# Four direct feed-forward pairs, block sums on DVE, SSD state updates in the second feed-forward block

## The chip, the cores and the metric

The kernel runs on one core of a Trainium2 chip. The metric is the device time of one execution in microseconds (us), as the median of several runs of the same program. Six engines with queues of their own matter: PE (matrix products, with PEld for its weight loads), DVE, ACT and POOL (elementwise work), and SP, which issues nearly all DMAs here. Each engine takes its instructions strictly in order and stands still at a wait.

## The reference

One step of a hybrid decoder layer on 512 prompt tokens and 8 sequences of 4 new tokens (544 columns in all), width 1024:

```python
x = x + 0.5 * swiglu(rmsnorm(x, n_f1), w_f1u, w_f1d)        # swiglu: (silu(g) * u) @ w_down, D_FF = 2816
m, new_conv, new_ssm, new_hg = mixer(rmsnorm(x, n_mix), ...)  # SSD heads and HGRN2 heads, then @ w_out
x = x + m
x = x + 0.5 * swiglu(rmsnorm(x, n_f2), w_f2u, w_f2d)
x = x + sigmoid(rmsnorm(x, n_ple) @ w_gate) * rmsnorm(p @ w_proj, ple_post)
y = rmsnorm(x, norm_final)
```

Beside `y` the new states come out. For the 8 sequences the new SSD state is h = h0 * decay + (sum of outer products of B and x), 2 groups x 8 sequences, each a tile of 128x512; the HGRN2 state is updated in the same way.

## The kernel before

Everything is kept transposed: 128 features on the partitions, 544 tokens in the free dimension, as two halves of 272. Every fp32 product is made of three matmuls (hi x hi, hi x lo, lo x hi). So an operand is first **cut**: ACT copies it to a rounded `hi` (line 245) and DVE subtracts to get `lo` (line 246). `body` runs `ffn` for the first block, the mixer, the W_o stage (lines 1169 to 1187), `ffn` for the second block, and a last gate.

**The feed-forward block (`ffn`, line 235)** has 22 gate/up pairs of 256 output features. A **direct pair** (`plain_mm`, line 330) takes 96 matmuls of 128x272, in four steps `kp` over K. All other pairs are made in a **period** (line 503) by seven products of sums of blocks, 84 matmuls (72 in the first period), at the price of sums and cuts of the weights (`w_s1` to `w_c4`) and of eight sums `t` of the input blocks. Before the change pairs 0 to 2 are direct and periods 3 to 21 follow. The input blocks `b` are x times the norm weight (`block`, line 314: a DVE `tensor_scalar` of 128x272 for each row block and half), cut into `bh`/`bl` (`put`; later ones are named `bx`). The eight sums `t` are made on POOL (lines 396 to 400), written behind pair 0. The tail of a direct pair (`plain_h`, line 365: scale, SiLU, two products, cut to `hh`/`hl`) is cut into steps that a table (`steps`, line 485) places in later work. The down products (`dn_run`, 24 matmuls) read `hh`/`hl` of four pairs at a time. In `ffn` the order on each engine is the order of the code (`pin`, line 62).

**In the W_o stage** 16 half slabs of 48 matmuls run. In the code, from the fourth half slab on, two or three state updates (lists `ups` and `begun`) are put between half slabs: 16 `ssm_update` (line 630: load `h0`, scale on POOL, mask `Bm` on DVE, one matmul of 128x512, add on DVE, store) and 16 `hg_update` (line 661, with `vb` on DVE ahead of its matmul). Here Tile's scheduler sets the order, and the first instructions of the second `ffn` can be mixed in.

## Time and profile before

| | us |
|---|---|
| median of 3 runs (1440.3 to 1443.42) | 1441.34 |
| the profiled execution | 1442.06 |
| its span (clock 0.983 of full speed on average) | 1440.2 |
| PE busy | 1386.6 (96%) |
| DVE busy | 1007.8 (70%) |
| ACT busy | 680.7 (47%) |
| POOL busy | 324.3 (23%) |

PE is busy nearly all the time, so the profile is read by its gaps: where PE stands still, what released it, and where its matmuls run at a lower granted clock. A timeline row is: start, duration, engine, line, operation, out<-in, count, and in brackets the idle time ahead and the releaser. On PE the first `ffn` runs from the start to about 399 us, the mixer to 835, the W_o stage to 951, the second `ffn` to about 1351.

### The profile page before, as it was taken

What the parts mean: (1) busy time and instruction counts of PE and PEld (TensorE: products, weight loads), DVE (VectorE), ACT (ScalarE), POOL (GpSimd) and SP (SyncE); (2) the same over time, 40 slices, a digit from 0 to 9 for tenths busy, and PEclk for the clock granted to TensorE, in tenths of its full rate; (3) what the DMA queues carried; (4) which work ended last, traced back from release to release, by engine and by line L of the source; (5) the groups of instructions that cost most, each with busy time, mean ns of one, the idle gap of its engine ahead of it and who ended that gap; (6) DMA issues with size and microseconds to landing.
All of it is one profiled execution on the core that took longest, in us unless ns stands there. A gap on an engine that the chain in (4) does not pass through costs nothing. (4 is left out here: it accounts for less than half of the span.)

```text
span 1440.2 us, 27177 instructions
## 1 busy us (share of the span) xinstructions
PE 1386.6 (96%) x11045; PEld 1340.8 (93%) x11045; DVE 1007.8 (70%) x1595; ACT 680.7 (47%) x1220; POOL 324.3 (23%) x285
## 2 busy tenths in 40 slices
PE   6989999999999999999999999979899999999997
PEld 6979999999999999999999799979799999999896
DVE  7687666666568887777775587785966666665465
ACT  5544444443443465555553373445444444343655
POOL 3243233232111100000001121233423223231100
PEclk9999999999999999999999999999999999999998
DMA  5223332332432422222222546762233233322311
GB/s 189 74 81 96 105 95 88 94 98 69 154 110 77 135 91 92 91 92 91 91 99 73 164 153 219 254 199 84 81 103 89 88 103 93 100 84 78 118 45 63
DMA packets 68191, 155.00 MB, mean 108 GB/s; under 512 B 8609, under 2 KB 15905, under 8 KB 68065
## 3 DMA queue, kind: packets, MB, share of 16 engines
q1 hardware_dynamic: 66480, 150.65, 33.1%
q10 hardware_dynamic: 1584, 2.61, 0.5%
q8 instruction: 87, 1.43, 0.4%
q14 instruction: 40, 0.32, 0.1%
HBM read 138.70 MB, written 14.52 MB: 106 GB/s over the span
## 5 line engine op out<-in xcount | busy, mean ns | idle before, releaser
L81 ACT CAST whi<-wraw 128x1024 fp32r<-128x1024 f32 (+2 forms) x140 | 132.5, 951 | 213.7 <-issue 85.7
L69 DVE TENSOR_TENSOR wlo<-wraw,whi 128x1024 fp32r<-128x1024 f32 (+2 forms) x140 | 161.5, 1157 | 92.0 <-ACT whi L81 87.8
L84 PE MATMUL ps_in<-xwh,whi 128*128 128x272 f32 x832 | 183.6, 297 | 0.0
L84 PE MATMUL ps_in<-xwh,wlo 128*128 128x272 f32 x832 | 175.5, 291 | 0.0
L84 PE MATMUL ps_in<-xwl,whi 128*128 128x272 f32 x832 | 173.5, 289 | 0.0
L84 PEld LDWEIGHTS ps_in<-xwh,whi 128*128 128x128 f32 x832 | 132.4, 188 | 8.5 <-issue 8.2
L81 ACT COPY s<-ps_s 128x272 f32<-128x272 f32 x114 | 43.7, 383 | 204.0 <-PE ps_s L84 204.0
L84 PEld LDWEIGHTS ps_in<-xwh,wlo 128*128 128x128 f32 x832 | 130.7, 189 | 2.9 <-issue 2.9
L84 PEld LDWEIGHTS ps_in<-xwl,whi 128*128 128x128 f32 x832 | 131.1, 189 | 1.5 <-issue 1.5
L69 POOL TENSOR_TENSOR wraw<-r,r 128x512 f32<-128x512 f32 x38 | 54.0, 1421 | 257.4 <-DVE r L69 257.4
L84 PE MATMUL ps_dn<-hl,dh 128*128 128x272 f32 x512 | 106.6, 290 | 3.8 <-DVE hl L69 3.8
L84 PE MATMUL ps_dn<-hh,dl 128*128 128x272 f32 x512 | 106.3, 289 | 0.1
L84 PE MATMUL ps_dn<-hh,dh 128*128 128x272 f32 x512 | 106.0, 288 | 0.0
L84 PE MATMUL ps_s<-bx,w3h 128*128 128x272 f32 x608 | 89.1, 289 | 7.2 <-ACT s L81 7.2
L84 PEld LDWEIGHTS ps_s<-bx,w3h 128*128 128x128 f32 x608 | 80.9, 188 | 8.2 <-ACT s L81 8.1
L84 PEld LDWEIGHTS ps_dn<-hl,dh 128*128 128x128 f32 x512 | 80.5, 189 | 4.3 <-DVE hl L69 4.3
L69 POOL TENSOR_TENSOR g<-g,r 128x544 f32<-128x544 f32 x38 | 67.3, 1772 | 63.7 <-ACT g L89 63.7
L84 PEld LDWEIGHTS ps_dn<-hh,dl 128*128 128x128 f32 x512 | 80.9, 189 | 0.5 <-DVE dl L69 0.5
L69 DVE TENSOR_TENSOR w3l<-r,w3h 128x1024 fp32r<-128x1024 f32 x40 | 51.3, 1282 | 42.1 <-ACT w3h L81 41.8
L84 PEld LDWEIGHTS ps_dn<-hh,dh 128*128 128x128 f32 x512 | 80.3, 189 | 0.0
L89 ACT ACT_TABLE_LOAD x55 | 70.6, 1283 | 3.3 <-DVE g L69 2.0
L69 POOL TENSOR_TENSOR s<-s 128x272 f32<-128x272 f32 x38 | 35.8, 943 | 117.7 <-ACT s L81 117.7
(381 smaller groups left out, 3605.1 us busy)
## 6 DMA issues: line engine op xcount, KB each, us to landing
wraw<-in_w_in SPq DMA_DIRECT2D x52, 512.0 KB, 3.3
r<-in_w1u SPq DMA_DIRECT2D x23, 512.0 KB, 4.3
r<-in_w2u SPq DMA_DIRECT2D x23, 512.0 KB, 4.4
dr<-in_w1d SPq DMA_DIRECT2D x32, 256.0 KB, 3.3
h<-in_hssm SPq DMA_DIRECT2D x32, 256.0 KB, 3.8
wraw<-in_w_o SPq DMA_DIRECT2D x16, 512.0 KB, 4.7
dr<-in_w2d SPq DMA_DIRECT2D x32, 256.0 KB, 3.3
wraw<-in_w1u SPq DMA_DIRECT2D x19, 256.0 KB, 3.3
```

The costliest lines, as they stand in the source:

```text
L69: pin((eng or V).tensor_tensor(out=out, in0=a, in1=b, op=op))
L81: pin(A.copy(out, a))
L84: pin(PE.matmul(out, w, x, **kw))
L89: ins = pin(A.activation(out=out, in_=in_, func=f, scale=scale, bias=bias, **kw))
```

## The change

Five edits, the first three in both feed-forward blocks:

1. Pair 3 is direct too: four direct pairs, then periods 4 to 21. Its weights are loaded ahead (`w3r`), and the tails of pairs 0 and 1 are finished within the direct part; those of pairs 2 and 3 lie in periods 4 and 5 (`steps`).
2. The eight sums `t` are made on DVE (`combo`), spread over pairs 1 and 2.
3. The second half of each block scaling is an ACT copy with a scale, the first stays on DVE.
4. `ssm_update` leaves the W_o stage, where one `hg_update` (once two) follows each half slab from the second on.
5. The SSD updates become a generator (`ssm_updates`) that the second `ffn` advances at four places of each period from 5 on (`aside`): load `h0`; scale by the decay (now on DVE) and `Bm`; the matmul; the add and the store.

```diff
@@ -234,3 +234,3 @@
 
-    def ffn(xs, nname, wu, wd, fp, ht, acc=None, load=None):
+    def ffn(xs, nname, wu, wd, fp, ht, acc=None, load=None, side=iter(())):
         pinned[0] = True
@@ -316,3 +316,7 @@
             for q in range(2):
-                ts(t[:, q], xs[2 * kp + q][:, half * HN:(half + 1) * HN], vc(nname, 2 * kp + q), ALU.mult)
+                src, n = xs[2 * kp + q][:, half * HN:(half + 1) * HN], vc(nname, 2 * kp + q)
+                if half:
+                    act(t[:, q], src, AF.Copy, scale=n)
+                else:
+                    ts(t[:, q], src, n, ALU.mult)
             blocks[kp, half] = t
@@ -383,3 +387,3 @@
             ks = slice(2 * kp, 2 * kp + 2)
-            b0, b1 = block(kp, 0), block(kp, 1)
+            b1, b0 = block(kp, 1), block(kp, 0)
             put(1 if kp < 2 else 2, kp % 2, b0)
@@ -395,7 +399,10 @@
             plain_mm(ps0, kp, w0h, w0l)
-        t = {(n, i): slot("t") for n, i in ((3, 1), (1, 0), (1, 1), (2, 0), (2, 1), (3, 0), (4, 0), (4, 1))}
-        for n, i in t:
-            x, y = {1: (blocks[i, 1], blocks[i, 0]), 2: (blocks[2 + i, 1], t[1, i]), 3: (blocks[i, 1], blocks[2 + i, 1]),
-                    4: (blocks[2 + i, 0], t[2, i])}[n]
-            tt(t[n, i], x, y, ALU.subtract, eng=G)
+        t = {}
+
+        def combo(n, i):
+            t[n, i] = slot("t")
+            x, y = {1: (blocks[i, 1], blocks[i, 0]), 2: (blocks[2 + i, 1], t.get((1, i))),
+                    3: (blocks[i, 1], blocks[2 + i, 1]), 4: (blocks[2 + i, 0], t.get((2, i)))}[n]
+            tt(t[n, i], x, y, ALU.subtract)
+
         w1h = [wtile(wp, "whi"), wtile(fp, "w3h", bufs=1)]
@@ -405,4 +412,6 @@
         w2r = [raw("r1", 8, 1), raw("r2", 8, 1)]
-        for q in range(2):
-            nc.sync.dma_start(w2r[q], wu[2][:, 8 * q:8 * q + 8])
+        w3r = [wp.tile([P, 8, P], F32, name="wraw", tag="wraw", bufs=2) for _ in range(2)]
+        for j, rw in ((2, w2r), (3, w3r)):
+            for q in range(2):
+                nc.sync.dma_start(rw[q], wu[j][:, 8 * q:8 * q + 8])
         done = [take(ps0, "g", None)]
@@ -410,2 +419,4 @@
         plain_mm(ps1, 0, w1h, w1l)
+        combo(1, 0)
+        combo(1, 1)
         if acc is None:
@@ -416,13 +427,14 @@
         plain_mm(ps1, 1, w1h, w1l)
-        put(5, 0, t[1, 0])
-        put(5, 1, t[1, 1])
         w2h = [wtile(wp, "whi") for _ in range(2)]
         w2l = [wtile(wp, "wlo") for _ in range(2)]
-        for q in range(2):
-            cut(w2r[q], w2h[q], w2l[q])
-        w_load(3)
+        cut(w2r[0], w2h[0], w2l[0])
+        combo(3, 0)
+        combo(3, 1)
+        cut(w2r[1], w2h[1], w2l[1])
         plain_mm(ps1, 2, w1h, w1l)
+        combo(2, 0)
+        combo(2, 1)
+        put(5, 0, t[1, 0])
+        put(5, 1, t[1, 1])
         plain_mm(ps1, 3, w1h, w1l)
-        put(6, 0, t[2, 0])
-        put(6, 1, t[2, 1])
         ps2 = two("ps_up")
@@ -433,8 +445,6 @@
         done.append(take(ps1, "g", None))
-        w_s1(3)
-        w_c2(3)
-        w_s3(3)
-        w_s4(3)
-        put(7, 0, t[3, 0])
-        put(7, 1, t[3, 1])
+        combo(4, 0)
+        combo(4, 1)
+        put(6, 0, t[2, 0])
+        put(6, 1, t[2, 1])
         pq = small()
@@ -444,8 +454,14 @@
         plain_mm(ps2, 1, w2h, w2l)
-        w_c1(3)
+        w3h = [wtile(wp, "whi"), wtile(fp, "w3h", bufs=1)]
+        w3l = [wtile(wp, "wlo"), wtile(fp, "w3l", bufs=1)]
+        cut(w3r[0], w3h[0], w3l[0])
+        put(7, 0, t[3, 0])
+        put(7, 1, t[3, 1])
         next(rg, None)
+        plain_mm(ps2, 2, w2h, w2l)
+        cut(w3r[1], w3h[1], w3l[1])
         put(4, 0, t[4, 0])
         put(4, 1, t[4, 1])
-        plain_mm(ps2, 2, w2h, w2l)
-        w_c3(3)
+        w_load(4)
+        plain_mm(ps2, 3, w2h, w2l)
         early = [plain_h(i, *done[i]) for i in range(2)]
@@ -453,5 +469,22 @@
             next(early[i % 2])
-        plain_mm(ps2, 3, w2h, w2l)
+        ps3 = [[small()[:, :HN] for _ in range(2)] for _ in range(2)]
+        plain_mm(ps3, 0, w3h, w3l)
         done.append(take(ps2, None, None))
         early.append(plain_h(2, *done[2]))
+        w_s1(4)
+        w_c2(4)
+        next(early[0])
+        next(early[1])
+        plain_mm(ps3, 1, w3h, w3l)
+        w_s3(4)
+        w_s4(4)
+        next(early[0])
+        next(early[1])
+        w_c1(4)
+        plain_mm(ps3, 2, w3h, w3l)
+        for i in (0, 1, 2, 2):
+            next(early[i])
+        plain_mm(ps3, 3, w3h, w3l)
+        done.append(take(ps3, None, None))
+        early.append(plain_h(3, *done[3]))
 
@@ -484,4 +517,4 @@
 
-        steps = {(3, 1): (0,), (3, 5): (0,), (3, 6): (0,), (4, 1): (1,), (4, 5): (1,), (4, 6): (1,), (4, 4): (2,),
-                 (4, 7): (2,), (5, 1): (2,), (5, 5): (2,), (5, 6): (2,)}
+        steps = {(4, 1): (2,), (4, 5): (2,), (4, 6): (2,), (4, 4): (3,), (4, 7): (3,), (5, 1): (3,), (5, 4): (3,),
+                 (5, 5): (3,)}
 
@@ -498,2 +531,6 @@
 
+        def aside(j):
+            if j > 4:
+                next(side, None)
+
         def gate(o):
@@ -517,2 +554,3 @@
                 gate(o)
+            aside(j)
             dn_out()
@@ -532,2 +570,3 @@
             dn_prep()
+            aside(j)
             product(a[:, :HN], w[6], X[6], False)
@@ -538,2 +577,3 @@
             dn_run()
+            aside(j)
             if j - 2 in GROUPS:
@@ -553,2 +593,3 @@
                 tail.append(last_slab(0))
+            aside(j)
             step(j, 5)
@@ -573,3 +614,3 @@
 
-        for j in range(3, NFF):
+        for j in range(4, NFF):
             period(j)
@@ -584,2 +625,3 @@
         ts_ = tail
+        aside(NFF)
         part(ts_[0], range(n - 1))
@@ -591,3 +633,7 @@
         h_parts(NFF - 1)
+        aside(NFF)
         part(ts_[1], range(n - 1))
+        aside(NFF)
+        for _ in side:
+            pass
         pinned[0] = False
@@ -629,6 +675,7 @@
 
-    def ssm_update(xp, g, b, st):
-        if b == 0:
-            xde = hs2(xp, "xde")
-            bkf = xp.tile([P, P], F32, name="bkf", tag="Bm", bufs=4)
+    def ssm_updates(fp, ht, tmp):
+        for g in range(2):
+            xde = ht("xde", F32)[:, :512]
+            bk = ht("bk", F32R)
+            bkf, Bh = f32(bk[:, :P]), bk[:, P:2 * P]
             for i in range(4):
@@ -636,25 +683,30 @@
                 nc.sync.dma_start(bkf[32 * i:32 * i + 32], bk_d[g])
-            xst = xp.tile([P, 512], F32R, name="xst", tag="xst", bufs=2)
-            Bk = xp.tile([P, P], F32, name="Bks", tag="Bks", bufs=2)
-            Bh = xp.tile([P, P], F32R, name="Bkh", tag="Bm", bufs=4)
-            A.copy(Bh, bkf)
-            A.copy(Bk, f32(Bh))
+            yield
+            yield
+            yield
+            xst = tmp()
+            Bk = fp.tile([P, P], F32, name="Bks", tag="Bks", bufs=1)
+            cp(Bh, bkf)
+            cp(xst, xde)
+            cp(Bk, f32(Bh))
+            tt(xst[64:], xde[64:], f32(xst[64:]), ALU.subtract)
             for i in (32, 96):
                 tt(Bk[i:i + 32], bkf[i:i + 32], f32(Bh[i:i + 32]), ALU.subtract)
-            A.copy(xst, xde)
-            tt(xst[64:], xde[64:], f32(xst[64:]), ALU.subtract)
-            st[g] = (xst, Bk)
-        xst, Bk = st[g]
-        h0 = hs2(xp, "h0")
-        nc.sync.dma_start(h0, hssm[g, b])
-        h3 = h0.rearrange("p (h q) -> p h q", q=64)
-        o = 64 + 16 * b + 8 * g
-        tt(h3, h3, cdk[:, o:o + 8].unsqueeze(2).to_broadcast([P, 8, 64]), ALU.mult, eng=G)
-        Bm = xp.tile([P, P], F32R, name="Bm", tag="Bm", bufs=4)
-        ts(Bm, Bk, cs("bmask")[:, b:b + 1], ALU.mult)
-        yield
-        pu = small()
-        PE.matmul(pu, Bm, xst, start=True, stop=True)
-        tt(h0, h0, pu, ALU.add)
-        nc.sync.dma_start(ssms_o[g, b], h0)
+            yield
+            for b in range(NB):
+                h0 = ht("h0", F32)[:, :512]
+                nc.sync.dma_start(h0, hssm[g, b])
+                yield
+                h3 = h0.rearrange("p (h q) -> p h q", q=64)
+                o = 64 + 16 * b + 8 * g
+                tt(h3, h3, cdk[:, o:o + 8].unsqueeze(2).to_broadcast([P, 8, 64]), ALU.mult)
+                Bm = fp.tile([P, P], F32R, name="Bm", tag="Bm", bufs=1)
+                ts(Bm, Bk, cs("bmask")[:, b:b + 1], ALU.mult)
+                yield
+                pu = small()
+                mm(pu, Bm, xst, start=True, stop=True)
+                yield
+                tt(h0, h0, pu, ALU.add)
+                nc.sync.dma_start(ssms_o[g, b], h0)
+                yield
 
@@ -1164,3 +1216,2 @@
                 for g in range(2):
-                    ups.append(lambda g=g, b=b: ssm_update(xp, g, b, st))
                     ups.append(lambda h=b, hf=g: hg_update(xp, h, hf, st))
@@ -1177,3 +1228,3 @@
                     next(g, None)
-                n = 0 if i < 3 else 3 - i % 2
+                n = 0 if i < 1 else 1 + (i == 8)
                 begun = [x() for x in ups[:n]]
@@ -1190,3 +1241,4 @@
         with tc.tile_pool(name="f2", bufs=1, reuse_waits="tile") as fp:
-            ffn(xs, "n_f2", w2u, w2d, fp, ring, acc2)
+            ffn(xs, "n_f2", w2u, w2d, fp, ring, acc2, side=ssm_updates(
+                fp, ring, lambda: xp2.tile([P, 512], F32R, name="xst", tag="sqa", bufs=1)))
 
```

DVE in the first `ffn`, from the last block of pair 0 to the cuts of pair 2's weights (`wlo<-r` and `w3l` are pair 1's and 2's weights, `sq` the squares for the norm), before:

```order
L69 TENSOR_TENSOR bl<-b,bh 128x544
L69 TENSOR_TENSOR wlo<-r_135,whi 128x1024
L69 TENSOR_TENSOR w3l<-r_139,w3h 128x1024
L69 TENSOR_TENSOR sq<-sq 128x544 x6
L69 TENSOR_TENSOR bl<-t,bh 128x544 x2
L69 TENSOR_TENSOR wlo<-r_319,whi 128x1024
L69 TENSOR_TENSOR wlo<-r_320,whi 128x1024
L69 TENSOR_TENSOR bx<-t,bx 128x544 x2
L69 TENSOR_TENSOR w5l<-r_420,w5h 128x512
```

and after the change:

```order
L69 TENSOR_TENSOR bl<-b,bh 128x544
L69 TENSOR_TENSOR wlo<-r_135,whi 128x1024
L69 TENSOR_TENSOR w3l<-r_139,w3h 128x1024
L69 TENSOR_TENSOR t<-b 128x544 x2
L69 TENSOR_TENSOR sq<-sq 128x544 x6
L69 TENSOR_TENSOR wlo<-r_303,whi 128x1024
L69 TENSOR_TENSOR t<-b 128x544 x2
L69 TENSOR_TENSOR wlo<-r_304,whi 128x1024
L69 TENSOR_TENSOR t<-b,t 128x544 x2
L69 TENSOR_TENSOR bl<-t,bh 128x544 x2
L69 TENSOR_TENSOR t<-b,t 128x544 x2
L69 TENSOR_TENSOR bx<-t,bx 128x544 x2
```

The sums `t`, which are POOL's before, stand between pair 1's squares and pair 2's weights, and the block scaling `b` is shorter.

DVE at the seam from the W_o stage to the second `ffn` (`xb<-ps_wo` are the last sums of the W_o stage, `s` and `h` the state updates, `vst`/`vb` the preparation of an `hg_update`; the rest is pair 0 of the second `ffn`), before:

```order
L69 TENSOR_TENSOR xb<-ps_wo,xb 128x544
L69 TENSOR_TENSOR s_11053<-s_11053,ps_s 128x512
L69 TENSOR_TENSOR h_11061<-h_11061,ps_s 128x512
L69 TENSOR_TENSOR sq<-sq 128x544
L69 TENSOR_TENSOR bl<-b,bh 128x544
L69 TENSOR_TENSOR vst<-vsf,vst 32x128 x2
L69 TENSOR_TENSOR vst<-vsf,vst 64x128
L69 TENSOR_TENSOR vb<-vst,cst 128x512
L69 TENSOR_TENSOR wlo<-wraw,whi 128x256
L69 TENSOR_TENSOR vb<-vst,cst 128x512
L69 TENSOR_TENSOR s_11076<-s_11076,ps_s 128x512
L69 TENSOR_TENSOR wlo<-wraw,whi 128x256
```

and after the change:

```order
L69 TENSOR_TENSOR xb<-ps_wo,xb 128x544
L69 TENSOR_TENSOR s_10907<-s_10907,ps_s 128x512
L69 TENSOR_TENSOR s_10974<-s_10974,ps_s 128x512
L69 TENSOR_TENSOR sq<-sq 128x544
L76 TENSOR_SCALAR b<-xb,vec 128x272
L69 TENSOR_TENSOR bl<-b,bh 128x544
L69 TENSOR_TENSOR wlo<-wraw,whi 128x256 x2
L69 TENSOR_TENSOR bl<-b,bh 128x544
L76 TENSOR_SCALAR b<-xb,vec 128x272 x2
L69 TENSOR_TENSOR bl<-b,bh 128x544
L69 TENSOR_TENSOR wlo<-wraw,whi 128x256 x2
L69 TENSOR_TENSOR bl<-b,bh 128x544
```

No update is prepared behind the last `xb` any more; two adds `s` are left, and what follows is all pair 0's.

DVE in the second `ffn`, one later period (`wlo<-wraw` is its c4 weights, `dl` a down slab), before:

```order
L69 TENSOR_TENSOR wlo<-wraw,whi 128x1024
L69 TENSOR_TENSOR dl<-dr,dh 128x512
L69 TENSOR_TENSOR g<-g,s_12026 128x272
L69 TENSOR_TENSOR g<-g,ps_s 128x272
L69 TENSOR_TENSOR hl<-g,hh 128x544
L69 TENSOR_TENSOR w5l<-r_12174,w5h 128x512
L69 TENSOR_TENSOR r_12260<-r_12174,r_12173 128x1024
L72 SCALAR_TENSOR_TENSOR xb<-ps_dn,xb 128x544
L69 TENSOR_TENSOR dl<-dr,dh 128x512
```

and after the change:

```order
L69 TENSOR_TENSOR wlo<-wraw,whi 128x1024
L69 TENSOR_TENSOR dl<-dr,dh 128x512
L69 TENSOR_TENSOR h_12184<-h_12184,cdk 128x512
L76 TENSOR_SCALAR Bm<-Bks,cst 128x128
L69 TENSOR_TENSOR g<-g,s_12022 128x272
L69 TENSOR_TENSOR g<-g,ps_s 128x272
L69 TENSOR_TENSOR hl<-g,hh 128x544
L69 TENSOR_TENSOR w5l<-r_12207,w5h 128x512
L69 TENSOR_TENSOR r_12298<-r_12207,r_12206 128x1024
L72 SCALAR_TENSOR_TENSOR xb<-ps_dn,xb 128x544
L69 TENSOR_TENSOR dl<-dr,dh 128x512
L69 TENSOR_TENSOR wlo<-r_12206,whi 128x1024
L69 TENSOR_TENSOR h_12184<-h_12184,ps_s 128x512
```

The scale and mask of an SSD update stand ahead of the products `g` of the pair before, and its add behind the cut of the next weights.

## Rows read from the trace of the kernel before

**Rows 1.** Waits of PE, whole span: line, waited for, us, times, longest.
```profile
PE ps_up L84 <- DVE bl L69: 9.8, 3, 4.3
...
PE ps_s L683 <- DVE vb L69: 6.2, 6, 1.7
```

**Rows 2.** Timeline of PE, first ffn, pair 0: start us, us, operation, [idle, releaser].
```profile
6.39 0.60 PE L84 MATMUL ps_up<-bh,whi 128*128 128x272 f32 x1 [6.39 <-ACT whi L81]
...
22.79 0.60 PE L84 MATMUL ps_up<-bl,whi 128*128 128x272 f32 x1 [4.08 <-DVE bl L69]
...
27.71 0.55 PE L84 MATMUL ps_s<-bh,whi 128*128 128x272 f32 x2
```

**Rows 3.** Timeline of DVE, first ffn, end of pair 0.
```profile
14.17 0.72 DVE L69 TENSOR_TENSOR bl<-b,bh 128x544 fp32r<-128x544 f32 x1
...
16.15 1.86 DVE L69 TENSOR_TENSOR bl<-b,bh 128x544 fp32r<-128x544 f32 x1 [0.17 <-ACT bh L81]
...
20.89 1.85 DVE L69 TENSOR_TENSOR bl<-b,bh 128x544 fp32r<-128x544 f32 x1
```

**Rows 4.** Timeline of POOL, first ffn, at the same time.
```profile
16.06 4.63 POOL L69 TENSOR_TENSOR t<-b 128x544 f32<-128x544 f32 x3 [15.08 <-DVE b L76]
```

**Rows 5.** Timeline of ACT, first ffn, start of the last K step of pair 0.
```profile
15.47 0.65 ACT L81 CAST bh<-b 128x544 fp32r<-128x544 f32 x1 [1.48 <-DVE b L76]
```

**Rows 6.** The page, part 5: a costly group of ACT.
```profile
L81 ACT COPY s<-ps_s 128x272 f32<-128x272 f32 x114 | 43.7, 383 | 204.0 <-PE ps_s L84 204.0
```

**Rows 7.** Windows: stretch, its us, busy us of each engine, granted clock, DMA share.
```profile
20.00:25.00 5.00, 2.21 (x10) 2.21 (x11) 5.00 (x4) 0.00 (x0) 5.00 (x4) 0.62 0.49 161
950.00:960.00 10.00, 6.30 (x39) 5.04 (x38) 9.81 (x20) 5.35 (x15) 1.82 (x2) 0.99 0.59 196
1060.00:1160.00 100.00, 100.00 (x798) 100.00 (x798) 67.36 (x85) 43.02 (x72) 31.16 (x24) 1.00 0.32 97
```

**Rows 8.** Timeline of PE, first ffn, periods 4 and 5.
```profile
65.80 0.67 PE L84 MATMUL ps_s<-bh,whi 128*128 128x272 f32 x4
...
76.86 1.27 PE L84 MATMUL ps_s<-bx,w3h 128*128 128x272 f32 x8 [1.88 <-ACT s L81]
...
81.41 0.77 PE L84 MATMUL ps_s<-bh,wlo 128*128 128x272 f32 x4 [1.77 <-DVE wlo L69]
...
92.17 1.26 PE L84 MATMUL ps_s<-bx,w3h 128*128 128x272 f32 x8 [0.95 <-ACT s L81]
...
97.89 0.52 PE L84 MATMUL ps_dn<-hl,dh 128*128 128x272 f32 x2 [1.91 <-DVE hl L69]
...
99.26 0.67 PE L84 MATMUL ps_s<-bh,whi 128*128 128x272 f32 x4
```

**Rows 9.** Timeline of PE, W_o stage to second ffn, pair 0 and start of pair 1.
```profile
950.63 0.39 PE L657 MATMUL ps_s<-xst,Bm 128*128 128x512 f32 x1
950.86 0.41 PE L84 MATMUL ps_up<-bh,whi 128*128 128x272 f32 x2
...
976.64 0.53 PE L84 MATMUL ps_s<-bh,whi 128*128 128x272 f32 x2
```

**Rows 10.** Timeline of PE, second ffn: start of period 4, end of the first down product.
```profile
1012.44 0.66 PE L84 MATMUL ps_s<-bh,whi 128*128 128x272 f32 x4
...
1046.89 0.43 PE L84 MATMUL ps_s<-bh,whi 128*128 128x272 f32 x1
```

**Rows 11.** Groups by form, 855 to 960: xcount | busy us, mean ns | idle before.
```profile
L69 DVE TENSOR_TENSOR h<-h,ps_s 128x512 f32<-128x512 f32 x16 | 11.0, 686 | 15.4 <-POOL h L69 7.5 <-issue 5.2 <-PE ps_s L657 2.8
...
L76 DVE TENSOR_SCALAR Bm<-Bks,cst 128x128 fp32r<-128x128 f32 x15 | 6.1, 414 | 0.0
...
L69 DVE TENSOR_TENSOR xst<-xde,xst 64x512 fp32r<-64x512 f32 x1 | 0.7, 690 | 0.0
```

**Rows 12.** Groups by form, 1060 to 1260, POOL.
```profile
L69 POOL TENSOR_TENSOR g<-g,r 128x544 f32<-128x544 f32 x12 | 22.1, 1846 | 8.7 <-ACT g L89 8.7
```

**Rows 13.** Timeline of DVE, second ffn, one steady period.
```profile
1166.83 1.23 DVE L69 TENSOR_TENSOR wlo<-wraw,whi 128x1024 fp32r<-128x1024 f32 x1 [2.21 <-ACT whi L81]
```

More of the change, by code (lines that the diff above doesn't have):

```diff
@@ L416, in ffn @@
         plain_mm(ps1, 1, w1h, w1l)
+        w2h = [wtile(wp, "whi") for _ in range(2)]
+        w2l = [wtile(wp, "wlo") for _ in range(2)]
+        cut(w2r[0], w2h[0], w2l[0])
+        combo(3, 0)
+        combo(3, 1)
+        cut(w2r[1], w2h[1], w2l[1])
+        plain_mm(ps1, 2, w1h, w1l)
+        combo(2, 0)
+        combo(2, 1)
         put(5, 0, t[1, 0])
         put(5, 1, t[1, 1])
-        w2h = [wtile(wp, "whi") for _ in range(2)]
-        w2l = [wtile(wp, "wlo") for _ in range(2)]
-        for q in range(2):
-            cut(w2r[q], w2h[q], w2l[q])
-        w_load(3)
-        plain_mm(ps1, 2, w1h, w1l)
         plain_mm(ps1, 3, w1h, w1l)
-        put(6, 0, t[2, 0])
-        put(6, 1, t[2, 1])
         ps2 = two("ps_up")
```

## The prediction

> **What bounds the kernel now.** I read the list of what PE waits for first, then PE's timeline around the longest waits, then the other engines at those times. In the steady periods there is nothing to win: from 1060 to 1160 us PE is busy 100.00 of 100 us with 798 matmuls at full clock, 0.1253 us each [rows 7]. That is the price of a matmul below, so a direct pair (96) is 12.0 us, a period (84) 10.5 us, a down product (24) 3.0 us. The time that can go lies at three kinds of place: the first direct pair of each block, where PE waits for DVE's `bl` (9.8 us in 3 waits), the state updates, where it waits for `vb` (6.2 us in 6) [rows 1], and the first periods, where it waits for what ends the direct pairs.
>
> Each wait costs twice. After a long one the matmuls go at half rate for a while: the granted clock in 20 to 25 us is 0.62 of full speed [rows 7], a mix of the levels 1.2 and 2.4 GHz. From 22.79 to 27.71 us, the last 22 matmuls of pair 0 take 4.92 us instead of 2.76 [rows 2].
>
> **A, first block, pair 0.** It runs from 6.39 to 27.71, with 4.08 us of waiting for `bl` ahead of 22.79 [rows 2]. DVE is the late one: its cut of 128x544 takes 0.72 at 14.17, but 1.86 and 1.85 at 16.15 and 20.89 [rows 3], and from 16.06 on POOL makes the sums `t` [rows 4]. An instruction that takes 2.6 times as long while POOL works on SBUF is a shared resource. The Trainium skill (SBUF — State Buffer, Who interferes with whom) says that a DVE instruction with two SBUF inputs and a POOL instruction that reads SBUF use one port, and that the later one stands still until the other is done; 1.86 against 0.72 agrees. With the sums gone from POOL, the stretch from 16.15 to 22.74 (two `bl`, two weight cuts) shrinks to about 2.2 us (twice 0.72 and about 0.8), so the last `bl` is there near 18.4, just as PE gets to it (18.71). The wait of 4.08 goes, and with it the slow clock behind it, 4.92 - 2.76 = 2.16: **6.2 us**. Two of four block scalings move to ACT, a copy of 128x272 at 0.38 [rows 6], 0.77 for a K step; ACT stands 1.48 us per K step waiting for DVE's `b` [rows 5], so that is covered. If it isn't and half of the wait stays, the term is 3.1.
>
> The eight sums cost DVE 8 x about 0.65 = 5.2 us (an addition of 128x512 is 0.69 [rows 11], and back to back they overlap). They lie beside pairs 1 and 2, 24 us of matmuls, where DVE has two thirds of its time in use. I take them at nothing. Were they late, the cuts of pair 2 would be: up to 2 us.
>
> **B, the added matmuls.** A direct pair has 12 matmuls more than a period, twice: 24 x 0.1253 = **-3.0 us**, certain.
>
> **C, first block, first periods.** From the start of period 4 (65.80) to the end of the first down product (99.26) are 33.46 us [rows 8] for 84 + 84 + 24 = 192 matmuls, 24.06 us: 9.4 lost. Of these 1.88 + 1.77 + 0.95 + 1.91 = 6.5 are the waits [rows 8]; the other 2.9 are slow clock. The pattern: the tail of a direct pair stands on DVE and ACT ahead of what the period needs, so ACT's copy `s`, which frees PE for the period's last product, and the cut of the next weights come late. Two such periods are in this stretch. In the new code pairs 0 and 1 end inside the direct part, period 4 has no period before it (like period 3 now, which loses next to nothing), and only period 5 is like these two. It keeps a wait for `s` between 0.95 and 3.65 (1.88 + 1.77); I take the middle, 2.3. The wait for `hl` stays, but for pair 3 instead of 2, six matmuls (0.75) later in the down product: 1.2. Of the slow clock half stays, 1.45. So 5.0 of 9.4 remain: **4.4 us**, between 1.0 (one of these periods at its worst, all of the slow clock) and 7.3 (2.1 remain).
>
> **D, the W_o stage.** Of 6.2 us for `vb`, 4.6 lie ahead of 951 us (the rest belongs to E) [rows 1]. Sixteen updates leave: on DVE 16 x (0.69 + 0.41) = 17.6 us [rows 11], on POOL their scaling, and of three updates between half slabs one is left. A `vb` then stands behind fewer others. I take **3.0**, between 1.5 and 4.6. The 16 matmuls of 128x512 (0.23 each, from 950.63 to 950.86 [rows 9]) leave here and come back in the second block: 3.7 - 3.7 = 0.
>
> **E, the seam.** From the first `ps_up` (950.86) to the first matmul of pair 1 (976.64) [rows 9] are 25.8 us for 96 matmuls and three updates, 12.7 us. DVE is the reason: it is busy 9.81 of 10 us from 950 to 960 [rows 7], with adds, preparations and cuts of the W_o stage, and then the contention of A comes again. After the change the order shows, between the last `xb` and pair 1's weights, two `s`, one `sq`, three `b`, four `bl` and four weight cuts of 128x256: 2 x 0.69 + 0.72 + 3 x 0.3 + 4 x 0.72 + 4 x 0.38 = 7.4 us, less than PE's 12.0. So PE sets the pace. The undisturbed part of pair 0 in the first block took 12.3 us (6.39 to 18.71) for 74 matmuls, by which 96 would take 16.0; with PE at full rate it is 12.0. I take 15.0: **10.8 us**, between 8 (18 us remain) and 13.
>
> **F, second block, first periods.** From 1012.44 to 1046.89 [rows 10] are 34.45 us, 10.4 lost. As in C 5.0 remain. In period 5 the preparation of the SSD updates (0.69 for `xst` [rows 11] and two of about 0.3) stands ahead of `hl`: 1.3 more. **4.1 us**, between 0.6 and 7.0.
>
> **G, the SSD updates in the steady periods.** Each adds on DVE scale 0.69 (priced as the add, the same shape), `Bm` 0.41 and add 0.69 [rows 11]: 1.8 us per period, 16 times. DVE is idle a third of the time (67.36 of 100 busy [rows 7]), 5.4 us of a period of 16.6 us (10.5 and two down products). The idle time is in the right place: 2.21 us ahead of the cut of c4 [rows 13], a few instructions in front of where scale and mask are put, and more behind. What they delay first is `g` and `hl` of the pair before, needed only some periods later, then ACT's copy `s`, which has a down product and two products (6 us) of time. The loads of `h0` stand in SP's queue one period ahead of their use, so DVE doesn't wait for them, and the stores go out behind the add. The cover is DVE's idle time; price **0**. The nearest bound from below is 0.5 per period, 8 us.
>
> **Sum.** 6.2 - 3.0 + 4.4 + 3.0 + 10.8 + 4.1 + 0 = 25.5 us. The profiled execution took 1442.06, its span and 1.9 us around it; the median is 0.7 less. 1441.34 - 25.5 = **1416 us**. With the good ends (6.2, 7.3, 4.6, 13, 7.0) the gain is 35.1: 1406. With all the bad ones (3.1, 1.0, 1.5, 8, 0.6, -8) it is 3: 1438; a part of them gives 1432.
>
> **Rivals.** *The updates stall every period.* Place: DVE's queue in the second block, behind `dl`. If the 1.8 us aren't covered, since DVE's gaps are waits for ACT that move along with the delay, then 16 x 1.8 = 29 us eat the 25.5: 1445, slower. It decides from 1.6 us per period. Against it: PE waits for nothing there now and DVE has 5.4 us. For it: POOL still makes `g` times r, 1.85 us each [rows 12], and a scale that meets it takes longer. By the rule of the Trainium skill (SBUF — State Buffer, Who interferes with whom) the scale would stand still for up to these 1.85 more; 3.6 us per period, all uncovered, would be 58 us and 1474. Chance 0.08.
>
> *Half of E and small stalls.* ACT still scales the last states `s` ahead of the casts of the second block; if their loads are late, the casts wait and E is 5 to 8, with C and F near their low ends: 1424 to 1438, say 1429. For it: at 950 us the DMA share is 0.59 [rows 7], twice the steady 0.32. Against it: half of that traffic is the SSD states, which leave. Chance 0.20.
>
> *The first periods lose nothing.* If the tails of pairs 2 and 3 fit fully, C and F gain 5.0 each over the forecast, and the preparation in period 5 finds cover: 1405. Chance 0.10.
>
> *No change.* If another engine sets the pace of pair 0 (ACT with its added copies) and periods 5 are worse than both before, the gain is 3 us or less. Chance 0.05.
>
> **Chances.** Forecast (1408 to 1424) 0.57, with the rivals 0.08, 0.20, 0.10 and 0.05. A measurement of this kernel can tell about 0.2%, 2.9 us. Faster by more 0.87, within 0.05, slower 0.08. The range 1406 to 1432 leaves out the slower rival, no change, and the outer parts of the others, some 2 in 10.
>
> **What would show it.** A: pair 1 starts near 21 us, and no DVE instruction beside it takes 1.86. C, F: one period with a wait for `s` instead of two. E: pair 1 starts some 15 us after the first `ps_up`. G: PE stays at 100 of 100 us from 1060 to 1160, with DVE near 78. I am wrong if PE there shows gaps that end with DVE or ACT, or if pair 0 of the second block waits for ACT's `bh`.

## The result and the profile after

The changed kernel takes 1418.76 us (1417.41 to 1419.13, 4 runs) against 1442.38 us for the kernel before in the same comparison: 23.6 us less, a ratio of 0.9831 with a 95% interval of 0.9808 to 0.9855. The forecast was 1416, a gain of 25.5. The profiled execution took 1418.97 us, its span is 1417.2 against 1440.2.

The waits of PE in the changed kernel, over the whole span (line, waited for, us, times, longest):

```profile
PE ps_up L84 <- ACT whi L81: 6.8, 1, 6.8
PE ps_s L84 <- ACT raw L81: 3.9, 2, 3.0
PE ps_s L84 <- ACT s L81: 3.5, 2, 2.4
PE ps_e L84 <- ACT pth L1259: 3.2, 1, 3.2
PE ps_dn L84 <- DVE hl L69: 2.5, 1, 2.5
...
PE ps_up L84 <- ACT bh L81: 0.3, 1, 0.3
```

Both lines of [rows 1] are gone: no wait for `bl`, none for `vb`. One line is new: `ps_s` waits for ACT's `raw`, 3.9 us in two places. PE's timeline around the places of [rows 2], [rows 8], [rows 9] and [rows 10]:

```profile
6.84 0.59 PE L84 MATMUL ps_up<-bh,whi 128*128 128x272 f32 x1 [6.84 <-ACT whi L81]
```

```profile
22.75 0.42 PE L84 MATMUL ps_s<-bh,whi 128*128 128x272 f32 x2
```

```profile
64.72 0.77 PE L84 MATMUL ps_s<-bh,whi 128*128 128x272 f32 x4 [0.89 <-ACT raw L81]
...
85.95 2.18 PE L84 MATMUL ps_s<-bx,w3h 128*128 128x272 f32 x8 [2.41 <-ACT s L81]
...
91.68 0.52 PE L84 MATMUL ps_dn<-hl,dh 128*128 128x272 f32 x2
...
92.28 0.66 PE L84 MATMUL ps_s<-bh,whi 128*128 128x272 f32 x4
```

```profile
935.38 0.41 PE L84 MATMUL ps_up<-bh,whi 128*128 128x272 f32 x2
...
947.38 0.41 PE L84 MATMUL ps_s<-bh,whi 128*128 128x272 f32 x2
```

```profile
988.87 0.77 PE L84 MATMUL ps_s<-bh,whi 128*128 128x272 f32 x4 [3.02 <-ACT raw L81]
...
1009.81 1.27 PE L84 MATMUL ps_s<-bx,w3h 128*128 128x272 f32 x8 [1.07 <-ACT s L81]
...
1016.86 0.52 PE L84 MATMUL ps_dn<-hl,dh 128*128 128x272 f32 x2 [2.49 <-DVE hl L69]
...
1017.47 1.04 PE L84 MATMUL ps_s<-bh,whi 128*128 128x272 f32 x4
```

The steady periods and DVE's cut at the end of pair 0, which answer to [rows 7] and [rows 3]:

```profile
1060.00:1160.00 100.00, 100.00 (x793) 99.72 (x793) 75.81 (x101) 42.88 (x73) 32.15 (x24) 1.00 0.42 127
```

```profile
16.38 0.73 DVE L69 TENSOR_TENSOR bl<-b,bh 128x544 fp32r<-128x544 f32 x1 [0.71 <-ACT bh L81]
```

From such starts the time can be split at the same seven places in every trace. *Pair 0* goes from the first `ps_up` to pair 1's first `ps_s`; *first periods* from there to the end of the first down product; *mixer*, which takes in the rest of the first block, to the first `ps_wo`; *W_o* to the first `ps_up` of the second block; *seam*, which is pair 0 there, to pair 1; then again *first periods*; *steady* to the first `ps_e`; *end* to the end of the span.

| us | pair 0 | first periods | mixer | W_o | seam | first periods 2 | steady | end |
|---|---|---|---|---|---|---|---|---|
| before | 21.3 | 71.6 | 735.8 | 115.8 | 25.8 | 70.3 | 304.3 | 89.0 |
| after | 15.9 | 69.5 | 735.8 | 107.3 | 12.0 | 70.1 | 308.5 | 91.2 |
| only updates moved | 21.1 | 71.8 | 736.1 | 107.2 | 17.6 | 71.8 | 308.2 | 91.0 |
| updates back in W_o | 14.8 | 69.1 | 735.9 | 118.8 | 20.3 | 69.2 | 303.5 | 91.6 |
| only sums and scalings | 15.2 | 71.4 | 736.1 | 114.5 | 20.3 | 70.3 | 304.3 | 89.0 |
| sums on POOL | 16.6 | 69.7 | 735.6 | 107.2 | 20.4 | 72.0 | 307.0 | 91.4 |
| SiLU in period 4 | 14.6 | 66.9 | 736.1 | 107.2 | 12.0 | 67.3 | 307.2 | 91.3 |
| + preparation later | 15.1 | 68.4 | 738.0 | 107.2 | 12.0 | 65.9 | 308.3 | 88.6 |
| + pair 3's tail later | 15.5 | 67.5 | 736.8 | 107.2 | 12.0 | 65.0 | 311.2 | 91.6 |
| more DVE work | 15.6 | 69.5 | 736.1 | 105.7 | 12.0 | 71.1 | 317.9 | 91.0 |
| scalings on DVE | 16.0 | 69.5 | 738.5 | 107.2 | 13.2 | 71.5 | 307.0 | 88.6 |
| after, second trace | 15.7 | 69.5 | 736.3 | 105.7 | 12.0 | 70.4 | 307.2 | 91.5 |

The rows below the second are the experiments that follow. A stage of one trace holds some noise: a stretch of 3.4 us at half rate costs up to 1.7 us, and where such stretches fall differs between traces. A little after the start of the W_o stage eight of the twelve traces have one and four have none, among them the kernel before and the second trace of the changed kernel. Its first trace, then its second:

```profile
843.50:847.50 4.00, 4.00 (x21) 4.00 (x21) 3.06 (x5) 2.71 (x6) 0.00 (x0) 0.58 0.22 70
```

```profile
843.50:847.50 4.00, 4.00 (x35) 4.00 (x35) 3.34 (x6) 3.15 (x6) 0.00 (x0) 1.00 0.21 70
```

### The profile page after: what moved, and what is told of

Its sections match the earlier page's. It is cut to its first block, busy times and chain, and to the rows that moved or that the text cites. A ratio compares the mean times of both kernels' runs of the same rounds, so it can differ in the third digit from the quotient of the medians.

```text
span 1417.2 us, 27123 instructions
## 1 busy us (share of the span) xinstructions
PE 1384.7 (98%) x11069; PEld 1342.9 (95%) x11069; DVE 1000.6 (71%) x1603; ACT 684.3 (48%) x1232; POOL 268.8 (19%) x245
## 4 chain that ended last, share of the span: by engine, by line
PE 92%; DVE 4%; ACT 2%; issue 1%; DMA 0%; SPq 0%; DVEq 0%; ACTq 0%
PE ps_in L84 22%; PE ps_s L84 19%; PE ps_dn L84 19%; PE ps_ed L84 10%; PE ps_wo L84 6%; PE ps_up L84 4%; PE ps_s L1344 3%; PE ps_e L84 1%; PE ps_s L946 1%; PE ps_s L943 1%; PE ps_pg L1344 1%; DVE wlo L69 1%; DVE raw L69 1%; ACT whi L81 1%; PE ps_s L1056 1%
## 5 line engine op out<-in xcount | busy, mean ns | idle before, releaser
L69 DVE TENSOR_TENSOR wlo<-wraw,whi 128x1024 fp32r<-128x1024 f32 (+2 forms) x140 | 156.9, 1125 | 82.5 <-ACT whi L81 78.5
L69 POOL TENSOR_TENSOR wraw<-r,r 128x512 f32<-128x512 f32 x36 | 48.7, 1353 | 263.4 <-DVE r L69 263.4
L84 PE MATMUL ps_s<-bx,w3h 128*128 128x272 f32 x576 | 85.2, 291 | 3.5 <-ACT s L81 3.5
L84 PEld LDWEIGHTS ps_s<-bx,w3h 128*128 128x128 f32 x576 | 77.6, 191 | 3.9 <-ACT s L81 3.9
L69 DVE TENSOR_TENSOR w3l<-r,w3h 128x1024 fp32r<-128x1024 f32 x38 | 46.8, 1230 | 34.7 <-ACT w3h L81 34.7
L69 POOL TENSOR_TENSOR r<-r,wraw 128x512 f32<-128x512 f32 x36 | 49.2, 1366 | 103.4 <-DMA wraw<-in_w2u 54.8
```

The source lines that it names most:

```text
L69: pin((eng or V).tensor_tensor(out=out, in0=a, in1=b, op=op))
L84: pin(PE.matmul(out, w, x, **kw))
```

## The experiments

**Only the SSD updates moved.** The kernel before with edits 4 and 5, the rest as it was:

```diff
-                    ups.append(lambda g=g, b=b: ssm_update(xp, g, b, st))
-                n = 0 if i < 3 else 3 - i % 2
+                n = 0 if i < 1 else 1 + (i == 8)
-            ffn(xs, "n_f2", w2u, w2d, fp, ring, acc2)
+            ffn(xs, "n_f2", w2u, w2d, fp, ring, acc2, side=ssm_updates(
```

> The kernel before with edits 4 and 5 alone: three direct pairs, sums on POOL, scalings on DVE, but the SSD updates in the second feed-forward block. My theory: the waits for vb in the W_o stage go (about 5 us), at the seam the part of the gain that DVE's adds and preparations held comes (6 to 7 of 13 us), and the wait for bl with POOL's sums beside it stays there; some 1 to 2 us are lost in period 5. About 1431 us. Rival: the updates alone made the seam late, then all of its 13 us come and it is near 1425. Other rival: POOL's sums alone made it late, then about 1438.

Measured: 1433.09 us, ratio 0.9937 (0.9915 to 0.9958). W_o and seam gain 8.6 and 8.2 us; the wait for `bl` at the seam stays, as PE's timeline of this kernel shows:

```profile
956.07 0.39 PE L84 MATMUL ps_up<-bl,whi 128*128 128x272 f32 x1 [3.83 <-DVE bl L69]
```

So the first theory holds, and the updates alone explain some six tenths of the seam's 13.8 us. The loss in period 5 came too: its wait for `hl` grows from 1.92 to 3.29 us, and the first periods of the second block take 1.5 us more.

**The SSD updates back in the W_o stage**, edits 1 to 3 kept:

```diff
+                    ups.append(lambda g=g, b=b: ssm_update(xp, g, b, st))
-                n = 0 if i < 1 else 1 + (i == 8)
+                n = 0 if i < 3 else 3 - i % 2
```

> The changed kernel with the SSD updates back in the W_o stage (edits 1 to 3 kept). My theory: 5 us of waits for vb come back, and about half of the seam's 13 us, less 1 to 2 us for the work that leaves period 5: about 1429 us, and no DVE cut beside pair 0 takes over 1 us. Rival: the seam needs only the sums off POOL: about 1423. Other rival: the seam is late by the updates alone: about 1434.

Measured: 1430.99 us, ratio 0.9919 (0.9892 to 0.9946). PE's waits of this kernel:

```profile
PE ps_s L729 <- DVE vb L69: 7.8, 6, 2.0
...
PE ps_up L84 <- DVE bl L69: 1.4, 2, 1.0
```

`vb` is back with 7.8 us, the seam is 20.3 us. As expected, but for the W_o stage, which gets 11.6 us longer and not 9. At 118.8 us it is 3 us longer than in the kernel before as well: this trace has two stretches of 3.4 us at half rate there (from 843.8 and 915.5 us), the trace before none.

**Only the sums on DVE and half of the scalings on ACT**, three direct pairs, updates in the W_o stage (the scalings as in the diff of the change):

```diff
-            tt(t[n, i], x, y, ALU.subtract, eng=G)
+            tt(t[n, i], x, y, ALU.subtract)
...
         plain_mm(ps1, 0, w1h, w1l)
+        combo(1, 0)
+        combo(1, 1)
...
         plain_mm(ps1, 2, w1h, w1l)
+        combo(2, 0)
+        combo(2, 1)
```

> The kernel before with edits 2 and 3 alone: three direct pairs, updates in the W_o stage, the sums on DVE spread over pairs 1 and 2, half of the scalings on ACT. My theory: pair 0 of the first block gains its 5 us, the seam about half of its 13, and the first periods lose as much as before: about 1431 us, some 2 us behind the same kernel with four direct pairs. Rival: the sums now load DVE ahead of the first periods, which is why a fourth direct pair is needed: over 1435.

Measured: 1433.21 us, ratio 0.9935 (0.9911 to 0.9959). Pair 0 is 6.2 us shorter, but it starts 1.4 us later in this trace, and its end is 4.8 us sooner; the seam is 5.5 us shorter. The first periods lose as much as before, no more: the rival falls. Together with the run on the moved updates the seam adds up: 25.8 - 8.2 - 5.5 = 12.1, and 12.0 are measured with both. That is the price of 96 matmuls, 12.0 us, so PE has no idle time left there.

**The sums on POOL again**, in the new places:

```diff
-            tt(t[n, i], x, y, ALU.subtract)
+            tt(t[n, i], x, y, ALU.subtract, eng=G)
```

> The changed kernel with the eight sums of each block back on POOL, in the same places of the code. My theory: POOL has nothing in front of them and makes them as soon as their blocks are there, beside the end of pair 0; the cuts of DVE take over 1.8 us again, PE waits for bl by some 4 us and its clock falls, in both blocks: about 1429 us. Rival: what mattered was the place in the code, and POOL's sums are now late enough: within 2 us of the changed kernel, 1419 to 1421.

Measured: 1427.11 us, ratio 0.9889 (0.9856 to 0.9923). Neither theory holds everywhere. In the second block the sums come beside the end of pair 0, as I had said. POOL, then DVE, then PE of this kernel:

```profile
944.26 6.16 POOL L69 TENSOR_TENSOR t<-b,t 128x544 f32<-128x544 f32 x4
```

```profile
946.19 3.04 DVE L69 TENSOR_TENSOR wlo<-wraw,whi 128x256 fp32r<-128x256 f32 x2
949.16 1.85 DVE L69 TENSOR_TENSOR bl<-b,bh 128x544 fp32r<-128x544 f32 x1
```

```profile
951.06 0.60 PE L84 MATMUL ps_up<-bl,whi 128*128 128x272 f32 x1 [4.17 <-DVE bl L69]
```

The seam is 20.4 us there, 8.4 more than in the changed kernel, which is about the whole loss. In the first block two sums ran early in pair 0 (the cuts beside them took 1.44 and 1.37 us). The third waited 16.6 us for a square of DVE, with which it shares its buffers; it and the rest ran beside pair 1, where they cost nothing to be seen, and pair 0 is 16.6 us, not 21. POOL there:

```profile
27.58 3.58 POOL L69 TENSOR_TENSOR t<-b 128x544 f32<-128x544 f32 x2 [16.63 <-DVE sq L69]
```

What makes POOL's sums expensive is the moment, not the engine.

**One SiLU behind the copies.** In the changed kernel period 4 waits for ACT's `raw`. The step of pair 2's tail that holds ACT moves into period 4:

```diff
-        for i in (0, 1, 2, 2):
+        for i in (0, 1, 2):
...
-        steps = {(4, 1): (2,), (4, 5): (2,), (4, 6): (2,), (4, 4): (3,), (4, 7): (3,), (5, 1): (3,), (5, 4): (3,),
+        steps = {(4, 1): (2, 2), (4, 5): (2,), (4, 6): (2,), (4, 4): (3,), (4, 7): (3,), (5, 1): (3,), (5, 4): (3,),
```

> The changed kernel with one step of pair 2's tail, its SiLU on ACT, moved from ahead of the copies of pair 3 into period 4, behind the cast of its c4 weights. My theory: period 4 waited (0.9 us in the first block, 3.0 in the second) since ACT stood in that SiLU's wait for DVE while the copies that free PSUM were queued behind it. Then the wait falls to what four copies take (under 1 us), the slow clock behind it goes too (1.7 us): 3 to 5 us faster than the changed kernel, about 1414.5. Rival: the copies are late by themselves, or the cast of w3h right behind them is what PE really needs: no more than 1 us, 1418.

Measured: 1411.88 us (1408.55 to 1414.07), ratio 0.9791 (0.9773 to 0.9810). That is 5.3 to 6.9 us less than the changed kernel (1417.21 and 1418.76 in its two series), faster than both kernels and a little more than expected. The intervals of the ratios just touch, but each of its four runs is faster than each of the changed kernel's nine. Both waits for `raw` are gone, not only shorter. How the chain looked in the changed kernel: DVE's product is slow beside POOL, ACT's SiLU waits for it, and the copies of pair 3 stand behind the SiLU. DVE, then ACT:

```profile
986.02 1.78 DVE L69 TENSOR_TENSOR raw<-raw,r 128x544 f32<-128x544 f32 x1
```

```profile
987.89 0.66 ACT L89 ACTIVATE raw<-raw 128x544 f32<-128x544 f32 x1 [5.10 <-DVE raw L69]
988.45 1.23 ACT L81 COPY raw<-ps_s 128x272 f32<-128x272 f32 x4
```

PE's period 4 starts at 988.87, when the first of these copies has freed its PSUM.

**The preparation one place later**, on top of the run before:

```diff
+            if g == 0:
+                yield
             xst = tmp()
```

> The kernel of the run before with the preparation of the first SSD group one place later, in period 6 instead of ahead of pair 3's cut in period 5. My theory: the wait for hl in the second block falls from 2.5 to below 1.3 us and the slow clock behind it gets shorter: 1.5 to 3.5 us faster than the run before, about 1412. Rival: hl is late by the weight cut ahead of it (2.3 us), not by the preparation: within 0.5 us.

Measured: 1412.61 us (1411.56 to 1413.48), ratio 0.9798 (0.9784 to 0.9813): not to be told apart from the run before, as the rival said. The wait for `hl` is there in both (1.26 and 1.18 us). But the rival's reason is only half of it. DVE in the second block, in the run before and then in this one:

```profile
1005.06 2.34 DVE L69 TENSOR_TENSOR wlo<-r,whi 128x1024 fp32r<-128x1024 f32 x1
1007.43 1.15 DVE L69 TENSOR_TENSOR xst<-xde,xst 64x512 fp32r<-64x512 f32 x1
1008.59 0.58 DVE L69 TENSOR_TENSOR Bks<-bk 32x128 f32<-32x128 f32 x2
1009.18 0.73 DVE L69 TENSOR_TENSOR hl<-raw,hh 128x544 fp32r<-128x544 f32 x1
```

```profile
1008.72 2.34 DVE L69 TENSOR_TENSOR wlo<-r,whi 128x1024 fp32r<-128x1024 f32 x1
1010.98 1.27 DVE L69 TENSOR_TENSOR hl<-raw,hh 128x544 fp32r<-128x544 f32 x1
```

From the start of the cut of c1 to the end of `hl` are 4.85 us with the preparation between them and 3.53 without it: `hl` is 1.3 us sooner, and the first periods of the second block are 1.4 us shorter. It is the same everywhere: 4.8 to 4.9 us in the second block of the seven traces with the preparation at this place, 3.5 in the four without it. The wait for `hl` didn't get shorter because PE came to it sooner as well, by 1.2 us counted from its wait for `s`. In the run before, PE goes at half rate between its waits for `s` and for `hl`; here it goes at full clock:

```profile
1004.00:1007.40 3.40, 3.40 (x18) 3.40 (x17) 3.39 (x3) 3.00 (x6) 2.78 (x2) 0.50 0.35 92
```

```profile
1006.50:1012.40 5.90, 4.63 (x33) 4.20 (x33) 5.90 (x6) 3.25 (x6) 3.40 (x2) 1.00 0.43 120
```

The wait that is left is the cut's. And the gain is mostly lost again: the preparation now stands ahead of a `dl`, for which PE waits 0.90 us at 1020.72.

**Pair 3's tail later as well:**

```diff
-        steps = {(4, 1): (2, 2), (4, 5): (2,), (4, 6): (2,), (4, 4): (3,), (4, 7): (3,), (5, 1): (3,), (5, 4): (3,),
-                 (5, 5): (3,)}
+        steps = {(4, 1): (2, 2), (4, 5): (2,), (4, 6): (2,), (4, 4): (3,), (4, 7): (3,), (5, 4): (3, 3, 3)}
```

> The kernel with SiLU in period 4 and the later preparation, and now the two products, the hi copy and the cut of pair 3's tail in one place of period 5, behind the down slab's cut and ahead of the cut of c1. My theory: in period 5 the last product waits 2.4 us for s since DVE makes pair 3's products ahead of the pair before's g, so ACT's hh and s come late; with g first that wait goes in both blocks, and as hl is cut ahead of c1 it is not later either; up to 1 us comes back as a wait for the cut of c1. 2 to 6 us faster than the run with the later preparation, about 1408. Rival: the work only changes places and the wait for hl grows by what the wait for s loses: within 1.5 us of it, 1411 to 1414.

Measured: 1414.95 us (1412.97 to 1415.90), ratio 0.9806 (0.9779 to 0.9832). The rival holds, and even it may have been too kind: this is 2.3 us more than the run with the later preparation, though the intervals overlap. The wait for `s` falls from 2.4 to 1.05 us, and the first periods are 0.9 us shorter in each block; but the steady part gets 2.9 us longer, since a wait for `xb` comes up, with slow clock behind it. PE in the second block (the last wait, for `dl`, was there in the run with the later preparation too):

```profile
1003.59 1.26 PE L84 MATMUL ps_s<-bx,w3h 128*128 128x272 f32 x8 [1.05 <-ACT s L81]
...
1009.07 0.51 PE L84 MATMUL ps_dn<-hh,dh 128*128 128x272 f32 x2 [1.16 <-ACT hh L81]
...
1018.04 0.49 PE L84 MATMUL ps_dn<-hh,dh 128*128 128x272 f32 x2 [1.36 <-DVE xb L72]
...
1019.68 0.82 PE L84 MATMUL ps_dn<-hh,dl 128*128 128x272 f32 x2 [0.90 <-DVE dl L69]
```

So a new order of this work mostly moves the waiting to another of its readers.

**More DVE work in the steady periods:**

```diff
+                for _ in range(3):
+                    h4 = h0.rearrange("p (h q) -> p h q", q=P)
+                    tt(h4, h4, ones.unsqueeze(1).to_broadcast([P, 4, P]), ALU.mult)
```

> The changed kernel with three more DVE products by ones on each h0 tile, 3 x 0.69 = 2.1 us more per period in 16 periods, at the place of the scaling; the values stay. My theory: DVE has 24 of 100 us idle, 4.0 us in a period of 16.6, so 2.1 more are covered as the 1.7 of the change were: within 3 us of the changed kernel, 1419 to 1422. Rival: what counts is the delay at this place, not the idle time; the products and cuts behind it come late for PE by most of the added time: 16 x 1 to 2 us, 1435 to 1450.

Measured: 1429.21 us, ratio 0.9918 (0.9901 to 0.9936). The steady part is 9.4 us longer, 0.6 for each of the 16 updates: neither theory. What was left idle did not cover 2.1 us more. The windows and a period of this kernel, DVE and then PE:

```profile
1060.00:1160.00 100.00, 98.28 (x758) 95.79 (x757) 92.53 (x115) 41.56 (x70) 33.12 (x23) 1.00 0.40 120
```

```profile
1108.68 1.78 DVE L69 TENSOR_TENSOR dl<-dr,dh 128x512 fp32r<-128x512 f32 x1
...
1111.09 2.14 DVE L69 TENSOR_TENSOR h<-h,ones 128x512 f32<-128x512 f32 x3
```

```profile
1119.36 0.52 PE L84 MATMUL ps_dn<-hh,dl 128*128 128x272 f32 x2 [0.33 <-DVE dl L69]
```

DVE is busy 92.53 of 100 us. From 75.81 this is more than the added products: the period is 17.7 us (1101.66 to 1119.36, the waits for `dl` of two periods), and 92.53% of that is 16.4 us, against 12.7 for 75.81% of 16.8. Of the 3.7 us only 2.1 are the products; the other instructions, shifted in time, meet POOL's: the cut `dl` takes 1.78 here and 0.69 in the changed kernel. From 1060 to 1260 us the mean of `dl` is 1.38 us here against 1.03, that of the two `wlo` 1.65 and 1.52 against 1.21 and 1.23.

**All scalings on DVE** (edit 3 undone, but for the order of the two halves):

```diff
-                if half:
-                    act(t[:, q], src, AF.Copy, scale=n)
-                else:
-                    ts(t[:, q], src, n, ALU.mult)
+                ts(t[:, q], src, n, ALU.mult)
```

> The changed kernel with both halves of the block scalings on DVE (edit 3 undone). My theory: the K steps of pair 0 come every 3.29 us before and after the change, since DVE and ACT take turns, and PE needs 3.0; the copy on ACT moved work and shortened little. Pair 0 gets up to 1 us longer in each block: 1419 to 1421. Rival: DVE's 0.6 us per K step count in full: 4 x 0.6 x 2 = 5 us, 1424.

Measured: 1420.95 us (1418.30 to 1422.33), ratio 0.9854 (0.9840 to 0.9870). Against 0.9831 (0.9808 to 0.9855) the intervals touch: a difference of about 2 us, not certain. The seam is 1.2 us longer, pair 0 of the first block no more than 0.1. So the scalings on ACT may be worth a little at the seam. The K steps do come every 3.29 us before and after the change, as I had said (cuts `bl` at 12.86 and 16.15, and at 13.09 and 16.38), but in this kernel every 3.83 (14.17 and 18.00). Edit 3 also scales the second half first (`b1, b0` for `b0, b1`), so that ACT's `bh` has to wait for all four scalings where they are DVE's: DVE waits 0.71 us for it in each step here, 0.17 in the kernel before. In pair 0 of the first block, then, the copies on ACT make good for what the new order costs and no more.

**The changed kernel again:**

> The changed kernel unaltered, for a second trace and a time beside the run above on the same chip: 1417 to 1420 us. The waits of PE are the same to 0.1 us; what can differ is how long the matmuls go at half rate behind a wait: pair 0 of the first block (15.9 us in the first trace, 14.6 to 16.0 in the other kernels with the sums on DVE) and the last stage (91.2 us, 88.6 to 91.6 in the others).

Measured: 1417.21 us (1415.66 to 1421.92), ratio 0.9836 (0.9809 to 0.9863). Not every wait repeats to 0.1 us: in period 5 of the second block `s` and `hl` cost 1.07 and 2.49 us in the first trace, 2.45 and 1.25 in the second. Their sum does (3.6 and 3.7). The wait for `raw` ahead of them is the same, 3.02 us in both; but behind it PE goes at half rate in the first trace and at full clock in the second. Late by that, it finds `s` sooner in the first:

```profile
990.30:993.60 3.30, 3.30 (x16) 3.30 (x15) 2.57 (x3) 1.66 (x3) 0.00 (x0) 0.50 0.00 0
```

```profile
986.00:992.00 6.00, 4.23 (x33) 4.23 (x34) 2.98 (x3) 4.98 (x10) 0.11 (x1) 1.00 0.08 31
```

The first periods of the second block take 70.1 and 70.4 us. So not each wait costs twice, as the prediction has it: slow clock may follow or not, and where it does, a later wait can shrink by what it cost.

## Why the prediction was right, point by point

Its time and range held, since errors of both signs in the terms nearly cancel: D and E gave 4.8 us more than forecast, the other terms and the end 7.2 less. That 25.5 us forecast meet 23.6 measured is in part luck. By the stages (a term is the difference of two stages, and the matmuls of an added pair or a moved update are taken out at the prediction's prices):

| term | forecast | measured | how |
|---|---|---|---|
| A, pair 0 | 6.2 | 5.0 | 21.3 - 15.9, less the start 0.45 later |
| B, added matmuls | -3.0 | -3.0 | 24 more matmuls (PE has 11069 now), at the prediction's price |
| C, first periods | 4.4 | 3.5 | 71.55 - 69.53 + 1.5 of B |
| D, W_o stage | 3.0 | 5.5 | 8.5, less 13 update matmuls that left this stage |
| E, seam | 10.8 | 13.1 | 13.8, less three update matmuls |
| F, first periods 2 | 4.1 | 1.7 | 0.2 + 1.5 of B |
| G, steady | 0 | -0.5 | -4.2, less 16 update matmuls that came (3.7) |
| end | not named | -2.2 | 89.0 - 91.2 |
| sum | 25.5 | 23.1 | span 23.0 shorter |

**A was right** in mechanism and size. The last cut ends at 18.4 as forecast, no cut takes 1.86, and nothing waits at the end of pair 0. The matmuls of pair 0 went at half rate (one every 0.227 us instead of 0.125) until 14 us in this trace and until 11 us in the one before; that explains the 1.2 us, for in two traces of experiments with half rate until 11 us (the updates back, the SiLU in period 4) pair 0 ends 6.5 and 6.6 us sooner than before. The second trace of the same kernel and six of the experiments with the sums on DVE give 14.6 to 15.7 us, where the forecast is 15.1; all scalings on DVE, the seventh, give 16.0. With the sums on POOL again, `bl` takes 1.1 to 1.85 us where the two meet, and 0.73 elsewhere. The rule of the Trainium skill (SBUF — State Buffer, Who interferes with whom), that a DVE instruction with two SBUF inputs contends with a POOL instruction that reads SBUF, agrees with these numbers.

**E was too small at one step.** The bound by PE, 12.0 us, was what came. I took 15 between this and 16.0 by the rate of the first block's start. That rate does not carry over: there PE comes from standing still and goes at half rate for its first 15 matmuls, until 11 us; at the seam it comes from the W_o stage at full clock. The forecast's 10.8 still counts 0.7 us for three updates that leave the seam; the 13.1 doesn't. How the gain splits is settled by two runs with a part of the change each: 8.2 us for the updates, 5.5 for the sums and scalings, of which the scalings may be 1.2. The rival of late states `s` on ACT didn't come.

**D was too small:** I left 1.6 of 4.6 us of waiting for `vb`, and none is left; 0.6 for an `xwl` ahead of it went too. The 5.5 are after a stretch at half rate that only the later trace has: by the second trace of the changed kernel, which has none (105.7 us), the term is 7.1.

**C and F failed at one step, the start of period 4.** It was to be like that of period 3 before, "which loses next to nothing". Before, pair 2 ahead of the first period stands in `ps_up`, the two big PSUM tiles. Now pair 3 is ahead of it and takes the four small ones (`small`), and the first thing that period 4 needs is one of these. So PE waits for ACT's copies of pair 3, 0.9 and 3.0 us. The run with the SiLU in the period shows that this is the cause: both waits are gone, and the two stages are 2.7 and 2.8 us shorter. In the first block that is more than the wait, since its trace lacks a stretch at half rate that the changed kernel's has at 41 us; the next run has the same edit and such a stretch (from 39 us), and is 1.1 us shorter there. Behind period 4's start all came as forecast. Of the 27.56 us from there to the end of the first down product (64.72 to 92.28), 180 matmuls are 22.6, so 5.0 are lost, and 5.0 was said; in the second block 6.0 of 28.60 (988.87 to 1017.47), where 6.3 was said. The wait for `s` is 2.41 us in the first block (forecast 2.3). And the preparation of the updates does make `hl` 1.3 us later, as the rows of DVE under the run with the later preparation show.

**G was right**, 0.5 us instead of 0 in the first trace and a gain of 0.8 in the second (307.2), so not to be told from 0: PE is busy 100.00 of 100 us, DVE 75.81 where 78 was named. Its reason was only half right. I had taken all of DVE's idle 5.4 us for cover. The run with more DVE work shows the end of it: 2.1 us more in each period cost 0.6 a period. The slower rival feared that a scale would meet POOL's work and stand still. None did: the 16 scales take 0.68 to 0.69 us each in the changed kernel.

**The fourth direct pair** may more than pay for its 3 us of matmuls, but that is not shown: between the run with the updates back in the W_o stage and the one without the fourth pair lie 2.2 us (1433.21 less 1430.99), and the two intervals overlap. The first periods are 2.3 and 1.1 us shorter in the traces.

## What to carry to other kernels

A helper engine that slows the busy one while both run costs by the moment when its work falls, so ask first when its queue will let it run: here eight sums cost 5 to 8 us at the end of the first pair, and nothing to be seen beside the second. When a step is made like its neighbour, check which buffers it holds as well as which engines it uses: the added pair took the PSUM tiles that its successor starts with, behind an in-order engine that stood in another wait. Idle time is cover only until the shifted instructions begin to meet others: here DVE's work grew by up to 3.7 us a period where 2.1 were added. And an equal wait in two traces doesn't show that what it waits for was equally late, if PE came to it at another clock: compare the operand's own times on its engine.
